# Memory between attention and mixer laid out anew, the first mixer weights split beside the last projection tiles, half of a combine moved into the attention

## The chip, the core and the metric

The kernel runs on one core of a Trainium2 chip. The metric is the device time of one execution in microseconds. Its engines are TensorE (PE in the profile; its weight loads are PEld), VectorE (DVE), ScalarE (ACT), GpSimd (POOL) and SyncE (SP, which only issues transfers here).

## What is computed

One layer of a decoder for 2048 tokens of width 1024. Four groups of heads read the same normalised input (RWKV, mLSTM, sliding-window attention and forgetting attention), one output projection follows, then a gated MLP whose gate goes through a causal convolution of width 3 ahead of the GELU. Cut to the steps after the head groups:

```python
h = concat(rwkv, mlstm, swa, fox) @ w_out          # output projection
x = x + rmsnorm(h, norm_mix_post)
u = rmsnorm(x, norm_ffn_pre)
g, up = split(u @ w_up)                            # 1024 -> 2 x 2816
f = gelu_tanh(causal_conv3(g)) * up
x = x + rmsnorm(f @ w_down, norm_ffn_post)
```

## The kernel before

Products are computed in pairs of float16 numbers (a high and a low part, three matmuls for one), so each operand is split: ACT writes the high part, DVE the rest. The scale of a split is a power of two from the largest absolute value, which is found by a maximum on DVE and an all-reduce over the partitions on POOL.

The stages that matter here are four. **Attention** (`fox`): forgetting attention, block by block; ACT's queue loads the keys into a rotating set of buffers (`ka`, `kb`). **Output projection** (`o_tiles`, from line 1475): 16 tiles of 128 tokens. A tile is 96 matmuls into `psg`, evacuated by ACT, scaled by `ot` (DVE and POOL), added to `x` on POOL (`xr`), normalised, and written into `V`, the mixer's input, by transposing transfers of SP. The scheduler lets eleven of the 16 tiles run beside the attention; five are left behind its last matmul.

**Mixer, first half** (`stage_n`): 22 steps j over slices of 128 hidden columns. `up_weights(j)` loads raw (1 MB), finds its maximum, and forms on POOL the sums `S` for a fast matrix product with seven products of half blocks; `up_split(j)` writes `Wup` (high part ACT, line 1633; low part DVE, line 1634); `ffn_up(p, j)`, for the token halves p = 0 and 1, runs 7 x 12 matmuls of 128x512 into `psa`, `psb`, `psc`, adds them up in `up` and `gb` (line 1654), applies convolution and GELU, multiplies with `up` on POOL (line 1688, F), stores F, and takes its maximum `mF` on DVE (line 1690). The split of the next weights is held back until the `up` add that `ffn_up` returns as its mark. `combine(p)` (from line 1546) prepares the block sums T of the mixer's input for half p: eight iterations of four additions on POOL, four subtractions on DVE, a cast on ACT and a subtraction on DVE.

**Mixer, second half** (`ffn_down`): 2112 matmuls with `Wd` and the stored F, scaled with the maxima `mD` of the down weights (line 1618, one load of `rd` and one reduction for each of 22 slices) and `mF`.

Each engine executes its queue in order. The order within a queue is set by a scheduler that goes by readiness; a wait for another engine holds what stands behind it on the same engine. In the kernel before, W0 and W1 are split once the pools of the output projection are closed, `raw` and `S` come from a pool of one buffer, and the 22 reductions `mD` stand in `up_weights`, with nothing that holds them back, so that DVE runs them early in the mixer.

Of the kernel before, what the change touches and what calls it, by code (L numbers as in the profile page):

```python
# [139 lines left out]
class Trunk:  # L140
# [794 lines left out]
    def stage2(self):  # L935
        with ExitStack() as ck, ExitStack() as co:
# [14 lines left out]
            with ExitStack() as cf:  # L951
                self.fox_pools(cf, 8, 4, 6, 4)
# [504 lines left out]
    def o_setup(self, ctx):  # L1457
        nc = self.nc
        self.U2 = [self.u2p.tile([P, 2, KT, C], F16, name=f"V{c}") for c in range(2)] + [None] * (NC - 2)
        self.so = self.small = self.pool(ctx, "small_o", bufs=2, side="right")  # L1460
        wp = self.pool(ctx, "wo", side="right")
        self.pso2 = self.pool(ctx, "ps_g", bufs=2, space=PSUM, side="right")
        self.row(wp, "post1")
        self.grow2 = self.gain_row(wp, 1)
# [98 lines left out]
    def stage_n(self):
# [4 lines left out]
        with ExitStack() as ctx:  # L1568
            self.small = self.sn
            self.raw = self.pool(ctx, "raw_n", bufs=1)  # L1570
            self.wp = self.pool(ctx, "w_n", bufs=2)
            self.wk = self.pool(ctx, "wk_n", bufs=2)
# [2 lines left out]
            W = {}
# [3 lines left out]
            self.Tc.append(tp.tile([P, 4, 2, 4, C], F16, name="T1"))  # L1579
# [2 lines left out]
            self.combine(1, lambda n: self.U2[1][:, n % 2, 0:4].rearrange("p k t -> p (k t)").bitcast(F32).rearrange("p (o t) -> p o t", o=4), self.Tc[1])
# [228 lines left out]
```

## Time and profile before

| | |
|---|---|
| median of 3 runs | 3085.03 us (3075.78 to 3097.76) |
| the profiled execution | 3085.7 us, of it 3083.9 us from the first to the last instruction |
| granted clock of TensorE, mean | 0.935 |
| PE busy | 2753.4 us (89%) |
| DVE, ACT, POOL busy | 1704.3, 1039.7, 844.4 us |
| longest chain by engine | PE 26%, issue 10%, DVE 5%, POOL 5%, DMA 3% |

A busy share says that an engine had work, not that it was what the others waited for. That is read from the idle time in front of an instruction and from the instruction that ended it, which the views of the trace give in brackets.

### The profile page before, as it was taken

To read this page: it belongs to the slowest core of one execution; us is meant where nothing else is said; L and a number is where in the kernel's file an instruction comes from. 1 tells how busy PE (TensorE), PEld (TensorE's weight loads), DVE (VectorE), ACT (ScalarE), POOL (GpSimd) and SP (SyncE) were. 2 spreads that over 40 slices of the span, in tenths; PEclk is the share of its full clock that TensorE was granted. 3 is DMA by queue.
4 is the path that set the end of the run, shared out by engine and by line. 5 is a ranking of instruction groups with operands and counts; after the bars stand their busy time and mean duration, and the time that the engine had idled before them with its cause. 6 is when DMAs were issued, how large, how long until landed. Compare 5 with 4: busy or idle time off the path is not lost.

```text
span 3083.9 us, 45114 instructions
## 1 busy us (share of the span) xinstructions
PE 2753.4 (89%) x17401; PEld 1657.9 (54%) x17401; DVE 1704.3 (55%) x3517; ACT 1039.7 (34%) x1844; POOL 844.4 (27%) x979
## 2 busy tenths in 40 slices
PE   5898998999888995998965578999999998999998
PEld 2455776777667873776754233444444443444443
DVE  6645664777765554567756665555555554622021
ACT  4423223445431233555643222222222222622020
POOL 2433221333233421222234322333333332010110
PEclk9998998999988996999987789999999999999999
DMA  9512333445442566575444231111111111832120
GB/s 262 118 60 83 82 102 89 103 105 137 116 131 72 130 168 173 136 143 124 106 93 116 83 121 69 55 55 55 55 55 55 55 55 52 286 117 96 48 86 21
DMA packets 341400, 313.70 MB, mean 102 GB/s; under 512 B 217600, under 2 KB 271232, under 8 KB 338368
## 3 DMA queue, kind: packets, MB, share of 16 engines
q1 hardware_dynamic: 265856, 238.42, 27.8%
q10 hardware_dynamic: 75328, 72.39, 8.1%
q8 instruction: 137, 2.24, 0.3%
q14 instruction: 79, 0.65, 0.1%
HBM read 187.86 MB, written 89.56 MB: 90 GB/s over the span
## 4 chain that ended last, share of the span: by engine, by line
PE 26%; issue 10%; DVE 5%; POOL 5%; DMA 3%; ACT 1%; ACTq 0%; POOLq 0%; SPq 0%; DVEq 0%
PE psd L1746 10%; PE psb L1651 7%; PE psc L1651 4%; PE psa L1651 4%; POOL S L1610 1%; POOL F L1688 1%; DMA rd<-in_w_dn 1%; POOL raw L1610 1%; DVE mF L1690 1%; DVE up L1654 1%; DVE mD L1618 1%; DVE gb L1654 1%; DMA wdr<-in_w_dn 0%; DVE V L1558 0%; POOL xo L1761 0%
## 5 line engine op out<-in xcount | busy, mean ns | idle before, releaser
L1651 PEld LDWEIGHTS <-Wup 128*128 128x128 f16 x3696 | 366.8, 99 | 558.4 <-issue 102.1
L1746 PE MATMUL psd<-Wd,f 128*128 128x512 f16 x2112 | 458.3, 380 | 7.2 <-ACT Wd L1731 7.2
L1651 PE MATMUL psb<-T,Wup 128*128 128x512 f16 x1584 | 383.4, 391 | 61.8 <-DVE up L1654 58.1
L1746 PEld LDWEIGHTS <-f 128*128 128x128 f16 x2112 | 207.1, 98 | 258.4 <-issue 5.8
L1651 PE MATMUL psa<-V,Wup 128*128 128x512 f16 x1056 | 249.7, 384 | 34.6 <-ACT Wup L1633 30.9
L308 PE MATMUL psg<-Wo,yt 128*128 128x256 f16 x512 | 146.9, 287 | 54.6 <-DMA yt<-hl 48.5
L1666 ACT ACTIVATE X<-psa,wm 128x512 f32<-128x512 f32 x44 | 30.2, 687 | 432.1 <-DVE p L220 254.7
L299 PE MATMUL psf<-U,hi_fm 128*128 128x256 f16 x576 | 163.6, 284 | 0.0
L298 PE MATMUL psf<-U,hi_fm 128*128 128x256 f16 x576 | 163.4, 284 | 0.0
L300 PE MATMUL psf<-U,lo_fm 128*128 128x256 f16 x576 | 163.3, 283 | 0.0
L310 PE MATMUL psg<-Wo,yt 128*128 128x256 f16 x512 | 144.6, 285 | 8.8 <-DMA yt<-hl 8.8
L1690 DVE TENSOR_REDUCE mF<-F 128x2 f32<-128x1024 f32 x44 | 53.7, 1221 | 176.2 <-POOL F L1688 176.1
L309 PE MATMUL psg<-Wo,yt 128*128 128x256 f16 x512 | 147.0, 287 | 0.0
L1754 DVE TENSOR_SCALAR od<-psd,sf 128x512 f32<-128x512 f32 x16 | 12.0, 750 | 234.0 <-PE psd L1746 229.5
L309 PE MATMUL psf<-lo_fv,U 128*128 128x256 f16 (+1 forms) x512 | 135.7, 273 | 2.7 <-DVE lo_fv L286 2.7
L308 PE MATMUL psf<-hi_fv,U 128*128 128x256 f16 (+1 forms) x512 | 135.6, 273 | 1.4 <-DVE gt L873 1.4
L1366 DVE TENSOR_REDUCE fmx<-psf 128x1 f32<-128x512 f32 (+3 forms) x160 | 96.0, 606 | 72.5 <-PE psf L1363 51.3
L310 PE MATMUL psf<-hi_fv,U 128*128 128x256 f16 (+1 forms) x512 | 135.5, 273 | 0.0
L1651 PE MATMUL psc<-T,Wup 128*128 128x512 f16 x528 | 132.4, 383 | 0.0
L1400 ACT ACTIVATE fP<-psf,ln2k 128x512 f32<-128x512 f32 (+3 forms) x160 | 98.0, 626 | 87.2 <-PE psf L1396 37.6
L1651 PE MATMUL psc<-V,Wup 128*128 128x512 f16 x528 | 122.4, 382 | 1.8 <-DVE up L1654 1.5
L1654 DVE SCALAR_TENSOR_TENSOR up<-psb,wm,X 128x512 f32<-128x512 f32 x88 | 65.8, 748 | 98.1 <-PE psb L1651 97.7
(452 smaller groups left out, 5984.6 us busy)
## 6 DMA issues: line engine op xcount, KB each, us to landing
raw<-in_w_up SPq DMA_DIRECT2D x22, 1024.0 KB
fD<-F SPq DMA_DIRECT2D x44, 512.0 KB
fr<-fD SPq DMA_DIRECT2D x88, 256.0 KB
rd<-in_w_dn SPq DMA_DIRECT2D x22, 512.0 KB
wdr<-in_w_dn ACTq DMA_DIRECT2D x22, 512.0 KB
zin<-zR SPq DMA_DIRECT2D x80, 128.0 KB
ka<-kA ACTq DMA_DIRECT2D x40, 256.0 KB
wst<-in_w_cm SPq DMA_DIRECT2D x17, 512.0 KB
```

What stands on the lines that cost most here:

```text
L298: nc.tensor.matmul(ps[:, sl], lhsT=hi[:, k, n0:n0 + nn], rhs=uh[:, k, sl], start=k == 0, stop=False)
L299: nc.tensor.matmul(ps[:, sl], lhsT=hi[:, k, n0:n0 + nn], rhs=ul[:, k, sl], start=False, stop=False)
L300: nc.tensor.matmul(ps[:, sl], lhsT=lo[:, k, n0:n0 + nn], rhs=uh[:, k, sl], start=False, stop=k == KT - 1)
L308: nc.tensor.matmul(ps, lhsT=uh[:, k, sl], rhs=hi[:, k, n0:n0 + nn], start=k == 0, stop=False)
L309: nc.tensor.matmul(ps, lhsT=uh[:, k, sl], rhs=lo[:, k, n0:n0 + nn], start=False, stop=False)
L310: nc.tensor.matmul(ps, lhsT=ul[:, k, sl], rhs=hi[:, k, n0:n0 + nn], start=False, stop=k == KT - 1)
L1366: nc.vector.tensor_reduce(out=mx[:, i, b:b + 1], in_=ps[:, :n], axis=AX.X, op=ALU.min)
L1400: nc.scalar.activation(out=e[:, o:], in_=ps[:, o:], func=AF.Exp, scale=-1.0, bias=self.ln2k)
L1651: nc.tensor.matmul(ps, lhsT=W[:, a, n, ks], rhs=rhs[u](b, k), start=first and k == 0 and i == 0, stop=k == 3 and i == 2, skip_group_check= ...
L1654: return nc.vector.scalar_tensor_tensor(out=out, in0=ps, scalar=un, in1=x, op0=ALU.mult, op1=ALU.add)
L1690: nc.vector.tensor_reduce(out=self.mF[:, 2 * p:2 * p + 2, j:j + 1], in_=F, axis=AX.X, op=ALU.max, apply_absolute_value=True)
L1746: nc.tensor.matmul(ps, lhsT=f[:, a, sl], rhs=Wd[j][:, b, ns], start=j == 0 and k == 0, stop=j == NF - 1 and k == 2)
```

## The change

It gives buffers of the mixer places of their own. `raw`, `S` and the first weight tile (`Wup0`) come from a pool that is opened before the last eight projection tiles; so the load and the split of W0 stand beside these tiles. The other buffers of `ffn_up` are fixed tiles that alternate. For the room, the attention has 7 key buffers instead of 8, the row `post2` is loaded in `ffn_down`, and one fewer of the down weights has an early place. The first half of `combine(0)` stands in the attention, its second half behind the tiles. The maximum of the down weights is a function of its own, `down_max`, which is held back to the same mark as the split.

```diff
-                self.fox_pools(cf, 8, 4, 6, 4)
+                self.fox_pools(cf, 7, 4, 6, 4)
...
+                    if c == 2:
+                        self.combine(0, lambda n: self.ow.tile([P, 4, W], F32, name="xs"), range(2))
             ck.close()
             keep = self.pool(self.ctx, "keep_n")
-            self.row(keep, "post2")
...
-            self.Tc = [u2b.tile([P, 4, 2, 4, C], F16, name="T0")]
+            self.Tc[0].append(u2b.tile([P, 4, 2, 2, C], F16, name="T0b"))
             self.tails = {}
-            for c in range(2, NC):
-                self.o_tiles(c)
-                if c == 2:
-                    self.combine(0, lambda n: self.ow.tile([P, 4, W], F32, name="xs"), self.Tc[0])
+            na = self.pool(self.cn, "n_a")
+            self.Wt = [na.tile([P, 2, 7, C], F16, name="Wup0")]
+            self.raw = na.tile([P, 4, C], F32, name="raw"), na.tile([P, 3, C], F32, name="S")
+            self.o_tiles(2)
+            self.o_tiles(3)
+            w = self.up_weights(0)
+            self.combine(0, lambda n: self.ow.tile([P, 4, W], F32, name="xs"), range(2, 4))
+            self.W = {0: self.up_split(0, w, None)}
...
+            self.Wt.append(self.pool(ctx, "n_w").tile([P, 2, 7, C], F16, name="Wup1"))
...
+            self.up, self.gb, self.F = two("up", [P, 2, C]), two("gb", [P, 2 * C + 2]), two("F", [P, 2, C])
+            self.rd = one("rd", [P, D])
...
-            for j in range(2):
-                W[j] = self.up_weights(j)
-                W[j] = self.up_split(W[j], None)
+            W[1] = self.up_split(1, self.up_weights(1), None)
...
                 mark = self.ffn_up(1, j, W[j])
-            W[2] = self.up_split(W[2], mark)
+                self.down_max(j, mark)
+            W[2] = self.up_split(2, W[2], mark)
+            self.down_max(2, mark)
             for j in range(2, NF):
                 if j + 1 < NF:
                     W[j + 1] = self.up_weights(j + 1)
                 mark = self.ffn_up(0, j, W[j])
                 if j + 1 < NF:
-                    W[j + 1] = self.up_split(W[j + 1], mark)
+                    W[j + 1] = self.up_split(j + 1, W[j + 1], mark)
+                    self.down_max(j + 1, mark)
                 mark = self.ffn_up(1, j, W[j])
...
-        d = self.wk.tile([P, D], F32, name="rd", tag="rd", bufs=1)
+        return R, S, m
+
+    def down_max(self, j, mark):
+
+        nc, d = self.nc, self.rd
         nc.sync.dma_start(out=d, in_=self.A["w_dn"][j])
-        nc.vector.tensor_reduce(out=self.mD[:, j:j + 1], in_=d, axis=AX.X, op=ALU.max, apply_absolute_value=True)
-        return R, S, m
+        with self.tc.issue_after(mark.ins):
+            nc.vector.tensor_reduce(out=self.mD[:, j:j + 1], in_=d, axis=AX.X, op=ALU.max, apply_absolute_value=True)
...
-            Wd = [None] * 3 + [wa.tile([P, 2, D], F16, name=f"Wd{j}") for j in range(3, 19)]
+            Wd = [None] * 3 + [wa.tile([P, 2, D], F16, name=f"Wd{j}") for j in range(3, 18)]
...
             fp = self.pool(ctx, "f_d")
+            self.row(fp, "post2")
```

What the queues hold at three places follows. First DVE in a late mixer step, from the mark (the `up` add) to the low part of the next weights, before:

```order
L1654 SCALAR_TENSOR_TENSOR up<-psb,wm,X 128x512
L220 TENSOR_SCALAR p_1_22960<-wm 128x1
L221 TENSOR_SCALAR p_1_22960<-p_1_22960 128x1
L222 RECIPROCAL p_1_22960<-p_1_22960 128x1
L1630 TENSOR_TENSOR wm<-p_1_22960,ug 128x1
L1654 SCALAR_TENSOR_TENSOR gb<-psb,wm,X 128x512
L1654 SCALAR_TENSOR_TENSOR gb<-psc,wm,gb 128x512
L1634 SCALAR_TENSOR_TENSOR Wup<-raw,p_1_22960,Wup 128x2048
```

and after:

```order
L1672 SCALAR_TENSOR_TENSOR up_19202<-psb,wm,X 128x512
L220 TENSOR_SCALAR p_1_22579<-wm 128x1
L1635 TENSOR_REDUCE mD<-rd 128x1
L221 TENSOR_SCALAR p_1_22579<-p_1_22579 128x1
L1672 SCALAR_TENSOR_TENSOR gb_19214<-psb,wm,X 128x512
L222 RECIPROCAL p_1_22579<-p_1_22579 128x1
L1646 TENSOR_TENSOR wm<-p_1_22579,ug 128x1
L1672 SCALAR_TENSOR_TENSOR gb_19210<-psc,wm,gb_19210 128x512
L1650 SCALAR_TENSOR_TENSOR Wup_19194<-raw,p_1_22579,Wup_19194 128x2048
```

The reduction `mD` and one `gb` add now stand ahead of the reciprocal, which ACT's split reads. The second place is DVE at the end of a step, where the three `up` adds and the maximum of F stand; one of the two kinds of step before:

```order
L1685 SCALAR_TENSOR_TENSOR F<-gb,pc,F 128x1024
L1686 SCALAR_TENSOR_TENSOR F<-gb,pc,F 128x1024
L1654 SCALAR_TENSOR_TENSOR up<-psb,wm,X 128x512
L1690 TENSOR_REDUCE mF<-F 128x2
L1654 SCALAR_TENSOR_TENSOR up<-psc,wm,up 128x512
L1654 SCALAR_TENSOR_TENSOR up<-psb,wm,X 128x512
```

and after, as in the other kind of before:

```order
L1700 SCALAR_TENSOR_TENSOR F_19222<-gb_19214,pc,F_19222 128x1024
L1701 SCALAR_TENSOR_TENSOR F_19222<-gb_19214,pc,F_19222 128x1024
L1705 TENSOR_REDUCE mF<-F_19222 128x2
L1672 SCALAR_TENSOR_TENSOR up_19202<-psb,wm,X 128x512
L1672 SCALAR_TENSOR_TENSOR up_19202<-psc,wm,up_19202 128x512
L1672 SCALAR_TENSOR_TENSOR up_19202<-psb,wm,X 128x512
```

The maximum moved ahead of the first `up` add. The third place is POOL beside the last projection tiles, after the change; `S` and `raw` are the block sums of W0 and W1, the line 1622 is the all-reduce (of W0's maximum, then of W1's), `xs` is `combine(0)`, `ot` and `xr` belong to a projection tile:

```order
L1622 ISA wm_19125<-wm_19125 128x1
L1623 ISA
L1623 TENSOR_TENSOR raw_18011<-raw_18011 128x512
L1623 TENSOR_TENSOR S_18012<-raw_18011 128x512
L1623 TENSOR_TENSOR S_18012<-raw_18011,S_18012 128x512
L1564 TENSOR_TENSOR xs_19165<-V0_14026 128x256 x2
L1564 TENSOR_TENSOR xs_19165<-V1_14027 128x256 x2
L1623 TENSOR_TENSOR S_18012<-raw_18011 128x512
L1622 ISA
L1622 ISA wm_19234<-wm_19234 128x1
L231 ISA
L231 TENSOR_TENSOR ot1_18415<-rsq_18560,mhalf_67 128x1
```

Before, one all-reduce (W0's) stood among these tiles and W1's behind them; now W1's stands there too, ahead of the scale `ot` of a tile. On PE, 36 of the matmuls of `ffn_up(0, 0)` stand between projection tiles now (17 behind the first of the last five tiles, 19 behind the second), where all of them stood behind the last tile before.

## Rows read from the trace of the kernel before

**Rows 1.** Page: busy us of an engine, share of the span, instructions.

```profile
PE 2753.4 (89%) x17401; PEld 1657.9 (54%) x17401; DVE 1704.3 (55%) x3517; ACT 1039.7 (34%) x1844; POOL 844.4 (27%) x979
```

**Rows 2.** Stretches: us, busy us by engine (PE, PEld, DVE, ACT, POOL), PEclk, DMA share, GB/s.

```profile
1200.00:1575.00 375.00, 328.99 (x2659) 251.73 (x2659) 244.32 (x478) 215.87 (x401) 95.55 (x87) 0.91 0.54 122
...
2150.00:2200.00 50.00, 50.00 (x233) 22.70 (x232) 27.85 (x31) 12.41 (x12) 15.05 (x12) 1.00 0.14 53
2200.00:2600.00 400.00, 386.20 (x1762) 173.39 (x1760) 218.26 (x237) 108.62 (x104) 130.48 (x101) 0.99 0.15 54
```

**Rows 3.** Waits of PE, 1576 to 1850: us in total, times, longest.

```profile
PE psg L308 <- DMA yt<-hl: 37.8, 3, 18.3
PE psa L1651 <- ACT Wup L1633: 30.9, 3, 16.3
```

**Rows 4.** Waits of PE, 1850 to 2610.

```profile
PE psb L1651 <- DVE up L1654: 39.5, 11, 9.9
```

**Rows 5.** Timeline of ACT: start, us, operation, [idle before, releaser]; splits of W3 to W21.

```profile
1864.59 2.00 ACT L1633 ACTIVATE Wup<-raw,p 128x2048 f16<-128x2048 f32 x1 [4.05 <-DVE wm L1630]
...
2102.68 1.99 ACT L1633 ACTIVATE Wup<-raw,p 128x2048 f16<-128x2048 f32 x1
...
2175.41 1.99 ACT L1633 ACTIVATE Wup<-raw,p 128x2048 f16<-128x2048 f32 x1
...
2256.07 1.99 ACT L1633 ACTIVATE Wup<-raw,p 128x2048 f16<-128x2048 f32 x1
...
2337.37 1.99 ACT L1633 ACTIVATE Wup<-raw,p 128x2048 f16<-128x2048 f32 x1
...
2559.96 1.99 ACT L1633 ACTIVATE Wup<-raw,p 128x2048 f16<-128x2048 f32 x1
```

**Rows 6.** Timeline of POOL in a slow mixer step.

```profile
2275.29 0.38 POOL L1608 PARTITION_ALL_REDUCE wm<-wm  x1 [6.08 <-DVE gb L1654]
2282.32 1.25 POOL L1610 TENSOR_TENSOR raw<-raw 128x512 f32<-128x512 f32 x1 [6.65 <-issue]
```

**Rows 7.** Timeline of DVE in the same step.

```profile
2255.30 0.15 DVE L220 TENSOR_SCALAR p<-wm 128x1 f32<-128x1 f32 x1
...
2288.60 1.22 DVE L1690 TENSOR_REDUCE mF<-F 128x2 f32<-128x1024 f32 x1 [10.38 <-POOL F L1688]
2289.74 0.74 DVE L1654 SCALAR_TENSOR_TENSOR up<-psb,wm,X 128x512 f32<-128x512 f32 x1
```

**Rows 8.** Timeline of PE: first mixer matmuls, a slow step, the last dozen.

```profile
1700.15 1.03 PE L1651 MATMUL psa<-V,Wup 128*128 128x512 f16 x2 [16.34 <-ACT Wup L1633]
...
1794.08 2.75 PE L1651 MATMUL psb<-T,Wup 128*128 128x512 f16 x12
...
1821.45 1.04 PE L1651 MATMUL psa<-V,Wup 128*128 128x512 f16 x2 [4.97 <-ACT Wup L1633]
...
2290.53 4.44 PE L1651 MATMUL psb<-T,Wup 128*128 128x512 f16 x12 [2.70 <-DVE up L1654]
...
2606.39 2.75 PE L1651 MATMUL psc<-V,Wup 128*128 128x512 f16 x12
```

**Rows 9.** Timeline of DVE: end of the last projection tile; last early `mD`.

```profile
1697.28 1.22 DVE L317 TENSOR_TENSOR hl<-xr,hl 128x1024 f16<-128x1024 f32 x1 [1.17 <-ACT hl L316]
...
1862.42 1.22 DVE L1618 TENSOR_REDUCE mD<-rd 128x1 f32<-128x1024 f32 x1 [2.59 <-DMA rd<-in_w_dn]
```

**Rows 10.** Combines: groups 1576 to 1800 (busy us, mean ns); ns min/median/max of one operation.

```profile
L1556 POOL TENSOR_TENSOR V<-V 128x256 f32<-128x256 f16 x32 | 24.2, 780 | 17.9 <-DVE T L1560 12.1 <-DMA V<-hl 5.8
L1558 DVE TENSOR_TENSOR V<-V 128x256 f32<-128x256 f32 x32 | 18.9, 604 | 31.2 <-POOL V L1556 31.0
L1560 DVE TENSOR_TENSOR T<-V,T 128x1024 f16<-128x1024 f32 x8 | 11.6, 1447 | 0.0
L1558 DVE TENSOR_TENSOR xs<-xs x32: 409/425/2385, 1399.8 to 1661.9; 128x256 f32<-128x256 f32 x32
```

**Rows 11.** Timeline of PE in the attention: the wait for a key block.

```profile
1213.98 0.76 PE L1362 MATMUL psf<-ka,qa 128*128 128x512 f32 x1 [8.93 <-DMA ka<-kA]
```

More of the change, by code (lines that the diff above doesn't have):

```diff
@@ L1459, in o_setup @@
         self.U2 = [self.u2p.tile([P, 2, KT, C], F16, name=f"V{c}") for c in range(2)] + [None] * (NC - 2)
+        self.Tc = [[self.u2p.tile([P, 4, 2, 2, C], F16, name="T0a")], []]
         self.so = self.small = self.pool(ctx, "small_o", bufs=2, side="right")
+        rp = self.pool(ctx, "wor", side="right")
+        self.row(rp, "post1")
+        self.grow2 = self.gain_row(rp, 1)
+        self.ow = self.pool(ctx, "ow", bufs=1, side="right")
         wp = self.pool(ctx, "wo", side="right")
         self.pso2 = self.pool(ctx, "ps_g", bufs=2, space=PSUM, side="right")
-        self.row(wp, "post1")
-        self.grow2 = self.gain_row(wp, 1)
         self.Wo = []
@@ L1544, in o_back, with combine @@
         return nxt
-    def combine(self, p, buf, T):
+    def combine(self, p, buf, ks):
         nc = self.nc
         B = [self.U2[2 * p + c][:, :, 4 * k:4 * k + 4] for c in range(2) for k in range(2)]
-        for k in range(4):
+        for k in ks:
+            T = self.Tc[p][k // 2]
             for t in range(0, C, W):
@@ L1569, in stage_n @@
             self.small = self.sn
[L1570 to L1572 removed]
+            self.Wt.append(self.pool(ctx, "n_w").tile([P, 2, 7, C], F16, name="Wup1"))
+            one = lambda n, shape: self.pool(ctx, "n_" + n).tile(shape, F32, name=n)
+            two = lambda n, shape: [one(n + str(i), shape) for i in range(2)]
+            self.X = one("X", [P, C])
+            self.up, self.gb, self.F = two("up", [P, 2, C]), two("gb", [P, 2 * C + 2]), two("F", [P, 2, C])
+            self.rd = one("rd", [P, D])
+            self.nup = 0
             self.psw = self.pool(ctx, "ps_w", bufs=2, space=PSUM)
             tp = self.pool(ctx, "t1_n", side="right")
[L1575 to L1579 removed]
+            W = self.W
+            W[1] = self.up_split(1, self.up_weights(1), None)
+            self.Tc[1] += [tp.tile([P, 4, 2, 2, C], F16, name=f"T1{i}") for i in range(2)]
             for j in range(2):
                 mark = self.ffn_up(0, j, W[j])
[L1582 removed]
+            self.combine(1, lambda n: self.U2[1][:, n % 2, 0:4].rearrange("p k t -> p (k t)").bitcast(F32).rearrange("p (o t) -> p o t", o=4), range(4))
             for j in range(2):
@@ L1603, in up_weights @@
         nc = self.nc
-        R = self.raw.tile([P, 4, C], F32, name="raw", tag="raw")
+        R, S = self.raw
         nc.sync.dma_start(out=R.rearrange("p s n -> p (s n)"), in_=self.A["w_up"][j])
@@ L1608, in up_weights @@
         nc.gpsimd.partition_all_reduce(m[:, 1:2], m[:, 0:1], P, RMAX)
-        S = self.raw.tile([P, 3, C], F32, name="S")
         gt = lambda o, x, y, op: nc.gpsimd.tensor_tensor(out=o, in0=x, in1=y, op=op)
@@ L1630, in up_split @@
             nc.vector.tensor_tensor(out=m[:, 2:3], in0=un, in1=self.ug[:, 1:2], op=ALU.mult)
-        W = self.wp.tile([P, 2, 7, C], F16, name="Wup")
+        W = self.Wt[j % 2]
         for o, x in ((slice(0, 4), R), (slice(4, 7), S)):
@@ L1681, in ffn_up @@
             nc.gpsimd.tensor_copy(out=self.tails[j], in_=gb[:, 2 * C:])
-        F = wk.tile([P, 2, C], F32, name="F")
         t = F.rearrange("p c n -> p (c n)")
@@ L1724, in ffn_down @@
             sd, sf = self.sd, self.sf
-            Wd = [wb.tile([P, 2, D], F16, name=f"Wd{j}") for j in range(3)] + Wd[3:] + [wb.tile([P, 2, D], F16, name=f"Wd{j}") for j in range(19, NF)]
+            Wd = [wb.tile([P, 2, D], F16, name=f"Wd{j}") for j in range(3)] + Wd[3:] + [wb.tile([P, 2, D], F16, name=f"Wd{j}") for j in range(18, NF)]
             def weights(j):
@@ L1785, in run @@
     def run(self):
-        self.cu, self.cr_, self.cf, self.c2, self.cb = (ExitStack() for n in range(5))
+        self.cu, self.cr_, self.cf, self.c2, self.cb, self.cn = (ExitStack() for n in range(6))
         self.setup()
```

18 lines of the change are left out of this document (9 added, 9 removed).

## The prediction

> **What bounds the kernel now.** I read the busy times first [rows 1]: PE works 89% of the span, so almost everything is decided by where PE waits. Then the table of stretches [rows 2]. It shows stages of different kinds. In the attention (1200 to 1575) PE is busy 329.0 of 375 us. In 2150 to 2200 it is busy 50.00 of 50: a mixer step at PE's own pace. Over 2200 to 2600 it is busy 386.2 of 400, so something else sets some of these steps. No edit touches the matmuls of the last product; I carry it over unchanged.
>
> Next the waits of PE. Between the end of the attention and the steady mixer the largest are two [rows 3]: 37.8 us for `yt`, the transposed input of a projection tile, and 30.9 us for the first weights (ACT Wup). In the steady mixer there is one kind, 39.5 us for `up` in 11 waits [rows 4].
>
> The order of the work says why. One mixer step (two `ffn_up`, 168 matmuls) is as long as the distance of two ACT splits of W. From the split of W3 (1864.59) to that of W21 (2559.96) there are 18 steps in 695.4 us, 38.6 each [rows 5]. They are of two kinds: 2102.68 to 2175.41 is two steps of 36.4 (PE's pace); 2256.07 to 2337.37 is two of 40.7. In the slow kind DVE's queue holds the second maximum `mF<-F` ahead of the `up` add. That maximum needs POOL's product F, and F stands in POOL's queue behind the all-reduce of the next weights: from the idle time ahead of the all-reduce to the next instruction, 6.08 + 0.38 + 6.65, POOL does nothing else for 13.1 us [rows 6], and three block sums follow ahead of F. `mF` then starts at 2288.60 after 10.38 us of an idle DVE, `up` at 2289.74 [rows 7], and PE goes on at 2290.53 after 2.70 us [rows 8]. PE pays twice: the dozen matmuls behind the stall lasts 4.44 us, an undisturbed one 2.75 (the row at 2606.39). In the fast kind `up` stands ahead of `mF`. So the slow step is a loop: mark (the `up` add) to split, to the next load of raw, to the all-reduce, to F, `mF`, `up`, mark.
>
> **The change part by part.**
>
> *1. Every step has the slow order, and a longer loop.* In the rows of the changed program all full steps on DVE have `mF` ahead of the three `up` adds (the order rows above show one); before about half had. POOL's order inside a step is the same, so F still stands behind the all-reduce. That alone puts 18 steps at 40.7 instead of 38.6: 18 x 2.1 = **+38 us**.
> To this comes the maximum of the down weights, `mD`. Before, 22 of them were run early; now one stands in each step right behind the mark, ahead of the reciprocal that ACT's split waits for, and a `gb` add moves ahead of the reciprocal too. Queued behind them: reciprocal, ACT split, DVE split, then SP's load of the next raw, the head of the loop. The price is in the trace, since one step of before has this very order: `mD` at 1862.42 to the split at 1864.59 is 2.17 us [rows 5, 9]; without it the first power instruction at 2255.30 to the split at 2256.07 is 0.77 [rows 5, 7]. That is **1.4 us** a step; its load waits are apart, because the next `rd` is loaded right behind the `mD` before it, a step ahead. Bounds: 0 (absorbed) to 2.2 (all of it). 18 x 1.4 = **+25 us**. A step is then 42.1, 18 steps are 758.
>
> *2. From the attention's end to W2.* Before, the last O matmul ended at 1700.15 - 16.34 = 1683.8, PE idled 16.34 us for W0, and the first use of W2 is at 1821.45 [rows 8]. Now W0 is split beside the last tiles: 36 of the 336 matmuls that precede W2 stand between O tiles, and the 16 us are gone. Against that, two all-reduces stand in POOL's queue there instead of one, the second ahead of the scale `ot` of a tile, with that tile's normalisation, transposes and later matmuls behind it. It can cost 0 to 13; I take 4, since PE waited for `yt` anyway in this stretch, 37.8 us [rows 3], and later tiles catch up. The mixer's remaining 300 matmuls at 50.00/233 = 0.215 us [rows 2] would end at 1683.8 + 4 + 64 = 1752 if nothing else waited. Something does: `combine(1)`, whose blocks the last 84 matmuls need. Its work in this stretch is 18.9 + 11.6 us on DVE and 24.2 on POOL [rows 10]; before it was drawn out to 1794 (the row at 1794.08 is the first matmul that needs all of it) by the all-reduces of W1 and W2 between its additions. Now both lie ahead of most of it. DVE reaches it when the last tile's row is normalised. Before, that was 15 us behind the last O matmul (`hl` at 1697.28 [rows 9]); now 4 later, behind a third all-reduce (13), and with the split of W1 between (two instructions of DVE and what they wait for, some 7): 1683.8 + 4 + 15 + 13 + 7 = 1723. An iteration is 30.5/8 = 3.8 us of DVE, with the mixer's adds between about 5.5; eight end at 1767. From its end to W2 before: 1821.45 - 1794.08 = 27.4, kept. W2 is used at 1794. Bounds: 1755 (PE's pace) and 1821 (no gain). Gain 27.
>
> *3. Attention.* One K buffer of eight is gone, so the fourth K load of the late blocks is issued only a few rows ahead of its use. Before, one load was waited for, 8.93 us [rows 11]. Bounds 0 and 9; I take 3. Half of `combine(0)` runs there: 16 POOL additions of 0.78 us and as many DVE subtractions [rows 10], beside a DVE busy 244 and a POOL busy 96 of 375 us [rows 2]. Hidden it costs nothing; were each addition to hold DVE on PE's path, 16 x 0.78 = 12.5. I take 2: nearer the lower end, since DVE has 131 us idle. Together **+5**. By the Trainium skill (SBUF — State Buffer, Who interferes with whom), a DVE instruction with two SBUF inputs and a GpSimd instruction that reads SBUF exclude each other for a whole instruction; by it the sum would take the 12.5 rather than 2, ten more. The trace agrees that some are held: the subtractions of this combine have a median of 425 ns and a longest of 2385 [rows 10].
>
> *4. W2 to W3.* Before 43.1 us (1821.45 to 1864.59), with a long wait for `up`. Now DVE's order in this one step has `mF` early, so PE is not held: 108 matmuls to the mark are 23.2 us at PE's pace, and some 2.5 to the split: 26. Gain 17.
>
> *5. End.* The last split to the last dozen: 2606.39 - 2559.96 = 46.4, kept, plus 1.4. The post2 row (512 KB) now is loaded as the last product begins: 0 to 3 us, I take 0 since its use is near the end. The Wo loads change place among SP's stores during the projections, far from their use: 0.
>
> **Sum.** W2 at 1794 + 5 = 1799; W3 at 1825; W21 at 2583; last dozen at 2631, against 2606.39: +24.6. The profiled execution took 3085.7 us (span 3083.9, 1.8 around it), the median is 3085.0: **3110 us**. About 1% (31 us) is what a measurement of this kernel can tell from no change; this lies just below.
>
> **Rivals.**
> *A, the sum* (chance 0.55), 3088 to 3132 with the bounds of 2 and 3.
> *B, mD is absorbed* (0.17). A step stays at 40.7: 25 less, 3085. For it: the split has had idle DVE around it. Against: the row of before that has this order.
> *C, the order does not bind* (0.10). If the slow steps came from something that the change removes, such as the early `rd` loads in SP's queue, all steps would run at 36.4: 18 x 5.7 = 103 less, 3007, faster. Against: the last early `mD` is at 1862.42 [rows 9], and steps are slow at 2214 to 2337 too.
> *D, the stretch between the stages gets worse* (0.18), the other side: the second all-reduce holds a tile its full 13 us, each later tile starts late, and combine(1) ends where it did. From W2 at 1815 on it decides: W2 at 1826 with the attention's 5 gives 3137, slower.
>
> **How the numbers follow.** Slower by over 1% (above 3116): 0.4 of A and nearly all of D, 0.22 + 0.17 = 0.39. Faster by over 1%: C and a little of B, 0.12. Within: 0.49. The range reaches from B with a W2 at 1780 (3066) to D (3138).
>
> **What would show it.** Step 1: the ACT splits of W in the steady mixer 42 us apart, DVE's `mF` with about 10 us idle before it in every step, PE waiting for `up` 18 times, about 5 us each with a slow dozen behind it. Step 2: no PE wait for W0, first use of W2 at 1794 to 1804. Step 3: a PE wait for K in 1300 to 1575, last attention matmul near 1580. Wrong would be: splits 36 to 37 apart (C), 40.7 (B), or W2 past 1815 (D).

## The result

The changed kernel takes 3131.18 us, the median of 4 runs (3120.62 to 3140.55), beside 3081.19 for the kernel before (4 runs): a ratio of 1.0152, 95% interval 1.0121 to 1.0182. It is slower by 1.5%. The time lies in the predicted range (3066 to 3138) and on the slower side, but 21 us above the 3110. The forecast was 25 us more than before and the measured change is 50, twice that; that it would stay within 1%, which I held likeliest, did not come.

The profiled execution of the changed kernel, the longest of its four, spans 3138.7 us against 3083.9. Cut at the points that the prediction used, the 54.8 us are:

| stretch | before | after | difference | predicted |
|---|---|---|---|---|
| start to the split of W3 | 1864.6 | 1830.1 | -34.5 | -39.6 |
| split of W3 to split of W21, 18 steps | 695.4 | 769.5 | +74.1 | +63 |
| split of W21 to the last dozen of `ffn_up` | 46.4 | 44.8 | -1.6 | +1.4 |
| last dozen to the end | 477.5 | 494.3 | +16.8 | 0 |

The first two rows are ACT's splits, which answer to [rows 5] (us from the start, duration, engine, instruction, idle time before it and what ended it):

```profile
1830.13 2.00 ACT L1649 ACTIVATE Wup<-raw,p 128x2048 f16<-128x2048 f32 x1 [1.28 <-DVE wm L1646]
...
2344.85 2.00 ACT L1649 ACTIVATE Wup<-raw,p 128x2048 f16<-128x2048 f32 x1 [1.28 <-DVE wm L1646]
...
2387.99 2.00 ACT L1649 ACTIVATE Wup<-raw,p 128x2048 f16<-128x2048 f32 x1 [1.28 <-DVE wm L1646]
...
2599.60 2.00 ACT L1649 ACTIVATE Wup<-raw,p 128x2048 f16<-128x2048 f32 x1 [1.36 <-DVE wm L1646]
```

(2599.60 - 1830.13)/18 is 42.75 us a step, the mean of 41.4 to 45.1; before it was 38.6, and 40.7 in the slow kind. The waits of PE from 1850 to the first product with `Wd` (total, times, longest) answer to [rows 4], where 11 waits made 39.5 us:

```profile
PE psb L1669 <- DVE up L1672: 76.8, 19, 6.8
```

One step on DVE answers to [rows 7]:

```profile
2377.93 1.22 DVE L1705 TENSOR_REDUCE mF<-F 128x2 f32<-128x1024 f32 x1 [10.80 <-POOL F L1703]
2379.07 0.74 DVE L1672 SCALAR_TENSOR_TENSOR up<-psb,wm,X 128x512 f32<-128x512 f32 x1
...
2385.18 0.75 DVE L1672 SCALAR_TENSOR_TENSOR up<-psb,wm,X 128x512 f32<-128x512 f32 x1 [4.58 <-PE psb L1669]
2385.85 0.14 DVE L220 TENSOR_SCALAR p<-wm 128x1 f32<-128x1 f32 x1
2385.91 1.21 DVE L1635 TENSOR_REDUCE mD<-rd 128x1 f32<-128x1024 f32 x1
```

and POOL in the same step answers to [rows 6]:

```profile
2355.43 2.36 POOL L1703 TENSOR_TENSOR F<-F,up 128x1024 f32<-128x1024 f32 x1
2364.55 0.38 POOL L1622 PARTITION_ALL_REDUCE wm<-wm  x1 [6.77 <-DVE gb L1672]
2371.66 1.25 POOL L1623 TENSOR_TENSOR raw<-raw 128x512 f32<-128x512 f32 x1 [6.73 <-issue]
2372.99 1.26 POOL L1623 TENSOR_TENSOR S<-raw 128x512 f32<-128x512 f32 x1
2374.34 1.26 POOL L1623 TENSOR_TENSOR S<-raw,S 128x512 f32<-128x512 f32 x1
2375.56 2.34 POOL L1703 TENSOR_TENSOR F<-F,up 128x1024 f32<-128x1024 f32 x1
```

The picture is the one forecast: in every step `mF` waits for F (9.7 to 13.4 us, 10.80 here), F stands on POOL behind the all-reduce and three sums, and PE pays some 4 us and then runs a slow dozen (2379.86 below, 5.07 us until the next dozen starts, where an undisturbed one takes 2.59):

```profile
2379.86 2.72 PE L1669 MATMUL psb<-T0a,Wup 128*128 128x512 f16 x6 [4.19 <-DVE up L1672]
2382.38 2.77 PE L1669 MATMUL psb<-T0b,Wup 128*128 128x512 f16 x6
2384.93 3.06 PE L1669 MATMUL psc<-V,Wup 128*128 128x512 f16 x12
```

The granted clock of TensorE says why the dozen is slow. Over these twelve matmuls, behind 4.19 us in which PE did nothing, it is 0.50, the lower of its two levels (1.2 GHz). Over the slow dozen of [rows 8], behind 2.70 us, it was 0.61. (Columns: stretch, its length, busy us and count of PE, PEld, DVE, ACT, POOL, granted clock, DMA share, GB/s.) Before:

```profile
2290.50:2294.90 4.40, 4.37 (x13) 1.69 (x13) 0.75 (x1) 0.00 (x0) 0.00 (x0) 0.61 0.04 16
```

and after:

```profile
2379.86:2384.90 5.04, 5.04 (x12) 1.78 (x12) 0.74 (x1) 0.00 (x0) 0.00 (x0) 0.50 0.03 13
```

The new loss is at the other end. After the last two dozens PE waits far longer for the first down weights than the 5.62 us before:

```profile
2644.44 2.75 PE L1669 MATMUL psc<-V,Wup 128*128 128x512 f16 x12
2663.23 8.13 PE L1762 MATMUL psd<-Wd,f 128*128 128x512 f16 x24 [16.04 <-ACT Wd L1747]
2673.59 5.34 PE L1762 MATMUL psd<-Wd,f 128*128 128x512 f16 x24 [2.23 <-ACT Wd L1747]
2681.76 58.61 PE L1762 MATMUL psd<-Wd,f 128*128 128x512 f16 x263 [2.83 <-ACT Wd L1747]
```

Of the 16.8 us, 10.4 are the longer way from the last dozen to the first product (18.79 against 8.37), 3.4 the two later waits (5.06 against 1.62), and 2.5 the slower pace of the products themselves (granted clock 0.65 over the first 24, 0.79 from 2681.7 to 2690.0; before 0.89 over the first 72).

### The profile page after: what moved, and what is told of

It reads as the page before. It is cut to its first block, busy times and chain, and to the rows that moved or that the text cites. A ratio compares the mean times of both kernels' runs of the same rounds, so it can differ in the third digit from the quotient of the medians.

```text
span 3138.7 us, 45022 instructions
## 1 busy us (share of the span) xinstructions
PE 2787.5 (89%) x17401; PEld 1668.8 (53%) x17401; DVE 1697.9 (54%) x3517; ACT 1041.4 (33%) x1844; POOL 801.5 (26%) x979
## 4 chain that ended last, share of the span: by engine, by line
PE 56%; issue 14%; DVE 11%; DMA 8%; POOL 7%; ACT 3%; SPq 1%; ACTq 0%; POOLq 0%; DVEq 0%
PE psd L1762 10%; PE psb L1669 8%; PE psc L1669 5%; PE psa L1669 4%; POOL S L1623 2%; PE psf L298 2%; PE psf L299 1%; POOL F L1703 1%; PE psf L300 1%; PE psf L308 1%; PE psf L310 1%; PE psf L309 1%; PE psb L682 1%; PE pss L1253 1%; PE pso L1415 1%
## 5 line engine op out<-in xcount | busy, mean ns | idle before, releaser
L1669 PEld LDWEIGHTS <-Wup 128*128 128x128 f16 x3696 | 373.5, 101 | 613.8 <-issue 192.0
L1669 PE MATMUL psa<-V,Wup 128*128 128x512 f16 x1056 | 251.2, 385 | 28.4 <-ACT Wup L1649 15.6
L1669 PE MATMUL psb<-T,Wup 128*128 128x512 f16 x792 | 190.1, 383 | 18.1 <-ACT T L1567 14.2
L1669 PE MATMUL psb<-T0a,Wup 128*128 128x512 f16 x396 | 120.9, 441 | 77.6 <-DVE up L1672 75.9
L308 PE MATMUL psg<-Wo,yt 128*128 128x256 f16 x512 | 144.7, 283 | 31.2 <-DMA yt<-hl 28.4
L1669 PE MATMUL psb<-T0b,Wup 128*128 128x512 f16 x396 | 116.4, 429 | 8.7 <-DVE T0b L1568 8.7
```

The lines of the kernel that those rows point to most:

```text
L308: nc.tensor.matmul(ps, lhsT=uh[:, k, sl], rhs=hi[:, k, n0:n0 + nn], start=k == 0, stop=False)
L1669: nc.tensor.matmul(ps, lhsT=W[:, a, n, ks], rhs=rhs[u](b, k), start=first and k == 0 and i == 0, stop=k == 3 and i == 2, skip_group_check= ...
```

## The experiments

All times are medians beside the kernel before on the same chip; "step" is the distance from the split of W3 to that of W21 in the profile, divided by 18.

| kernel | time us | ratio (95% interval) | step |
|---|---|---|---|
| changed kernel | 3131.2 | 1.0152 (1.0121 to 1.0182) | 42.75 |
| e1 changed, mF late | 3048.3 | 0.9872 (0.9845 to 0.9899) | 37.9 |
| e2 before, mF late | 3050.7 | 0.9884 (0.9843 to 0.9924) | 36.8 |
| e3 changed, mD not held | 3073.2 | 0.9969 (0.9949 to 0.9990) | 38.7 |
| e4 changed, loads late | 3132.9 | 1.0145 (1.0112 to 1.0177) | 42.6 |
| e5 changed, mF and mD behind the splits | 3160.9 | 1.0262 (1.0224 to 1.0301) | 44.5 |
| e6 changed, mD behind the splits | 3173.9 | 1.0287 (1.0251 to 1.0323) | 45.0 |
| e7 changed, down weights elsewhere | 3122.2 | 1.0127 (1.0098 to 1.0157) | 42.9 |
| e8 changed, line of the combine moved back | 3138.0 | 1.0180 (1.0150 to 1.0210) | 42.6 |
| e9 = e1 + mD behind the splits + e7 | 3027.1 | 0.9816 (0.9771 to 0.9860) | 36.8 |
| e10 = e1 + e7 | 3044.1 | 0.9882 (0.9844 to 0.9920) | 37.8 |
| e11 = e9 + e4 | 3022.1 | 0.9794 (0.9768 to 0.9819) | 36.9 |
| e12 changed, no all-reduce of the up weights | 2982.1 | 0.9667 (0.9636 to 0.9697) | 36.3 |

### Is it mF that holds the loop?

**e1** queues the maximum of a block's F behind the next block's marked add; **e2** is the same edit on the kernel before.

```diff
...
-        nc.vector.tensor_reduce(out=self.mF[:, 2 * p:2 * p + 2, j:j + 1], in_=F, axis=AX.X, op=ALU.max, apply_absolute_value=True)
+        late = self.late
+        self.late = lambda: nc.vector.tensor_reduce(out=self.mF[:, 2 * p:2 * p + 2, j:j + 1], in_=F, axis=AX.X, op=ALU.max, apply_absolute_value=True)
+        if late:
+            with self.tc.issue_after(mark.ins):
+                late()
```

> The changed kernel with one edit: the maximum mF of a block's F is queued on DVE behind the mark of the next block, so that in no step it stands ahead of the up adds. Loop theory (mF behind POOL's all-reduce holds up, and up holds PE): a step falls from 42.75 us to PE's pace, 36.3 (up to 38 if the split, now later behind mF and mD, is waited for), so 18 steps give back 85 to 116 us: 3015 to 3046 us. Rival (the step is set by something else, such as the load of raw or the split behind mD): steps stay at 41 to 43, 3100 to 3130 us.

> The kernel before with the same single edit (mF behind the next mark). Loop theory: its slow steps of 40.7 us fall to 36.3, the mean of 18 steps from 38.6 to 36.3, 41 us less: about 3040 us. Rival (the slow steps of before had another cause): no change, 3081 us.

Measured 3048.3, 83 us less than the changed kernel, and 3050.7. Every step of e1 is 37.8 to 38.4 us. PE's wait for `up` is all but gone from its waits after 1850 (one of 0.8 us is left); two short waits for the new weights are in its place:

```profile
PE psb L1671 <- ACT Wup L1651: 7.7, 18, 0.4
PE psa L1671 <- DVE Wup L1652: 6.9, 18, 0.4
```

So the place of `mF` on DVE is the whole wait for `up`, 4.9 of the 6.45 us by which a step of the changed kernel is longer than PE's pace of 36.3, and a loss of the kernel before as well. With `mF` late no difference between the two kernels is left: 3048.3 and 3050.7, on one chip. The times came 2 us above the expected range and some 10 us above the expected value.

### What does mD cost?

**e3** lets the scheduler place `mD` again:

```diff
-        with self.tc.issue_after(mark.ins):
-            nc.vector.tensor_reduce(out=self.mD[:, j:j + 1], in_=d, axis=AX.X, op=ALU.max, apply_absolute_value=True)
+        nc.vector.tensor_reduce(out=self.mD[:, j:j + 1], in_=d, axis=AX.X, op=ALU.max, apply_absolute_value=True)
```

> The changed kernel with one edit: the maxima mD of the down weights are not held behind the mark, so DVE runs them early as before; by DVE's order 9 of 18 steps then have up ahead of mF again. Theory (order of mF and price of mD make the loop's loss): the mean step falls from 42.75 to 38.6, 75 us less, against 10 to 15 us more where the 22 maxima crowd the start: 3066 to 3076 us. Rival (only the price of mD, 1.4 us a step, counts, the order does not): 25 us less, about 3106 us.

Measured 3073.2. With `mD` free the order of DVE is mixed again, as before: steps of 36.1 to 36.5, of 40.6 to 42.4, and a few between. The slow ones, 41.3 on the mean, are 1.5 below the 42.75: about that is what the held `mD` adds to a slow step. But holding it also did the larger thing: with it, the scheduler put `mF` first in all steps. The rest of the change, taken together, is no loss: with `mD` free the changed kernel is 0.3% faster than the kernel before (0.9949 to 0.9990).

### Is it the order on DVE, or the all-reduce behind it?

**e6** held `mD` behind the second DVE split of the next weights, **e5** besides it one `mF` of a step behind that split and the other behind the next marked add.

```diff
-            nc.vector.scalar_tensor_tensor(out=W[:, 1, o], in0=x, scalar=sc, in1=W[:, 0, o], op0=ALU.mult, op1=ALU.subtract)
+            self.split = nc.vector.scalar_tensor_tensor(out=W[:, 1, o], in0=x, scalar=sc, in1=W[:, 0, o], op0=ALU.mult, op1=ALU.subtract)
...
-                    self.down_max(j + 1, mark)
+                    self.down_max(j + 1, self.split)
+                self.flush(self.split if j + 1 < NF else mark)
```

(`flush` issues the `mF` that waits; that line is e5's alone.)

> The changed kernel with both reductions held behind the splits of the next weights on VectorE: the maximum mF of a block after the next block's marked up add, the maximum mD of the raw down weights after the two vector splits. In its order VectorE then has per step: powers, wm, gb, the two vector splits, mD, mF, and only then the wait for GpSimd. Theory A (the steps are slow because mF and mD stand ahead of the work that starts the split): the steps from the split of the weights 3 to that of the weights 21 fall from 42.75 to 36.3 us, as the quick steps of the kernel before (36.3 to 36.5); 18 x 6.45 = 116 us off 3131: 3010 to 3025. Rival B (only mF counts, the 37.8 us that its deferral alone left are set by the wait for the Wup split, not by mD): steps 37.5 to 38, 3043 to 3053, as with mF alone deferred.

> The changed kernel with one word changed: mD of the raw down weights is held behind the second vector split instead of behind the marked up add. The price of mD in its place was worked out as 1.65 us a step (slow steps 42.75 with it, 41.1 where it was not held). By that price alone the steps are 41.1 us and the time 3131 - 18 x 1.65 = 3101. But in the order the scheduler then also puts mF behind the two up adds of the next block (it still stands ahead of the marked add). Theory A (what counts is that PE's up adds do not wait behind mF): the steps come under 39 us, PE's wait for the up adds goes from 76.8 us to under 25, and the time is 3020 to 3065. Rival B (mF anywhere ahead of the mark costs the same): 41 us a step, 3095 to 3108.

Both went the wrong way, to 3160.9 and 3173.9, and neither theory had this. The order of e5 on POOL shows why, beside that of e1:

```profile
2318.82 1.27 POOL L1631 TENSOR_TENSOR S<-raw 128x512 f32<-128x512 f32 x1 [5.97 <-DMA raw<-in_w_up]
2326.06 0.38 POOL L1630 PARTITION_ALL_REDUCE wm<-wm  x1 [5.97 <-issue]
2333.51 1.25 POOL L1631 TENSOR_TENSOR raw<-raw 128x512 f32<-128x512 f32 x1 [7.08 <-issue]
...
2336.07 2.34 POOL L1711 TENSOR_TENSOR F<-F,up 128x1024 f32<-128x1024 f32 x1
```

In e1 the F of this half block stands ahead of S and of the all-reduce:

```profile
2289.96 2.35 POOL L1705 TENSOR_TENSOR F<-F,up 128x1024 f32<-128x1024 f32 x1 [2.16 <-ACT F L1704]
2295.09 1.27 POOL L1625 TENSOR_TENSOR S<-raw 128x512 f32<-128x512 f32 x1 [2.79 <-DMA raw<-in_w_up]
2302.45 0.38 POOL L1624 PARTITION_ALL_REDUCE wm<-wm  x1 [6.08 <-issue]
```

In e5 DVE does the two reductions and the maximum of the next raw ahead of the convolution's second step, so that F is ready later and the all-reduce goes first (read from the orders; no run sets it apart). Its `mF` then waits longer than in the changed kernel, ahead of two `gb` adds:

```profile
2338.44 1.22 DVE L1714 TENSOR_REDUCE mF<-F 128x2 f32<-128x1024 f32 x1 [12.13 <-POOL F L1711]
2339.58 0.74 DVE L1680 SCALAR_TENSOR_TENSOR gb<-psb,wm,X 128x512 f32<-128x512 f32 x1
```

and PE's wait after 1850 has another name and is larger than 76.8:

```profile
PE psb L1677 <- DVE gb L1680: 101.6, 18, 7.5
```

In e6 POOL's order is the same: F behind the all-reduce, `mF` waiting 11.8 to 15.2 us for it, mostly ahead of the two `gb` adds, and PE's waits are 93.5 us for `gb` and 22.1 for `up`.

Which add stands behind `mF` is not what counts; that any add does, while F is behind the all-reduce, is. **e12** takes the all-reduce itself away (each partition's own maximum stands in its place, so the result is not the layer's):

```diff
-        nc.gpsimd.partition_all_reduce(m[:, 1:2], m[:, 0:1], P, RMAX)
+        nc.gpsimd.tensor_copy(out=m[:, 1:2], in_=m[:, 0:1])
```

> The changed kernel with the maximum over the partitions left out where the up weights are scaled: GpSimd copies each partition's own maximum in place of the all-reduce (some 13 us of GpSimd a step with what stands idle around it). So part of the computation is missing. VectorE's order keeps mF directly ahead of the up adds in every half step. Theory A (an up add waits for mF, mF for GpSimd's product F, and that product stands on GpSimd behind the all-reduce and the sums of raw): with the all-reduce gone the same order has steps under 38.5 us, TensorE's wait for the up adds goes from 76.8 us to under 15, and the time is 3131 - 18 x 4.3 or more = 3054 or less. Rival B (the order on VectorE costs the time by itself, mF and mD ahead of the adds and the split, whatever GpSimd does): steps of 41 us and more, 3100 to 3131.

Measured 2982.1. DVE's order still has `mF` ahead of the `up` adds, and `mD` behind the mark, but `mF` now waits 3.56 us, and PE has a single wait for `up` after 1850, of 0.8 us:

```profile
2283.96 1.22 DVE L1705 TENSOR_REDUCE mF<-F 128x2 f32<-128x1024 f32 x1 [3.56 <-POOL F L1703]
2285.09 0.74 DVE L1672 SCALAR_TENSOR_TENSOR up<-psb,wm,X 128x512 f32<-128x512 f32 x1
...
2291.57 0.75 DVE L1672 SCALAR_TENSOR_TENSOR up<-psb,wm,X 128x512 f32<-128x512 f32 x1 [4.95 <-PE psb L1669]
...
2292.29 1.21 DVE L1635 TENSOR_REDUCE mD<-rd 128x1 f32<-128x1024 f32 x1
```

Steps of 36.3 us are 14 dozens of 2.59, PE's own pace. So neither `mF` first nor `mD` costs PE anything by itself: both cost only while the all-reduce makes the way from split to mark the longer one.

### The end: order, place or loads?

**e4** issues the row `post2` and the first `xo` loads behind the sixth split of `Wd`; **e7** gives `Wd0` a place beside the early loads and moves the others. First e7's edit:

```diff
-            Wd = [None] * 3 + [wa.tile([P, 2, D], F16, name=f"Wd{j}") for j in range(3, 18)]
+            Wd = [None] * 3 + [wa.tile([P, 2, D], F16, name=f"Wd{j}") for j in range(3, 15)]
...
+            w0 = s0.tile([P, 2, D], F16, name="Wd0")
...
```

and e4:

```diff
-            self.row(fp, "post2")
...
-                nc.scalar.activation(out=W[:, 0], in_=r, func=AF.Copy, scale=sd[:, 1:2])
+                hi = nc.scalar.activation(out=W[:, 0], in_=r, func=AF.Copy, scale=sd[:, 1:2])
+                if j == 5:
+                    with self.tc.issue_after(hi.ins):
+                        self.row(fp, "post2")
+                    self.xo_mark = hi
...
-                nc.scalar.dma_start(out=x, in_=self.x2[r])
+                with self.tc.issue_after(self.xo_mark.ins):
+                    nc.scalar.dma_start(out=x, in_=self.x2[r])
```

> The changed kernel with one edit: the load of the post2 row and the loads of xo (2 MB together) are issued behind the sixth split of the down weights instead of ahead of the first; ACT's order is otherwise the same. The last product starts 18.8 us behind the mixer's last dozen in the changed kernel, 8.4 before, and PE waits 21.1 us for Wd in all instead of 7.2. Theory A (these loads delay the all-reduce ahead of the last product and the loads of wdr): about 10 us less, 3121 us. Theory B (ACT's order, the first split behind a GELU and three f, and wdr buffers that wait for the last F): no change, 3131 us.

> The changed kernel with other places in memory for the down weights: the first (Wd0) stands beside the early loads, where raw and S end with the last split, instead of under the up weights that the last products still read; the twelve that stood lowest stay, the rest move up by three. In the order ScalarE then splits Wd0 right after the last F, ahead of f and of the GELU, and issues the next load of wdr behind the first two f; nothing else moves on any engine up to there. Theory A (the 14 us that the tail lost against the kernel before are the order on ScalarE that the new memory brought): PE's first wait for Wd falls from 16.0 us to about 10.5, the waits of TensorE for Wd together from 21.1 to under 13, and the time by 6 to 10 us to 3121 to 3125. Rival B (the wait is that for the maxima on GpSimd, whose all-reduce came 3 us later than before): the first wait stays over 14 us and the time at 3128 to 3134. The loop's steps stay at 42.7 us either way.

e4 took 3132.9, no change, though POOL stood idle 6.67 us ahead of the all-reduce of the maxima instead of 9.17: PE still waited 14.46 for `Wd`, and more behind it. ACT's queue shows what was in the way. In the kernel before, the split of `Wd0` followed the scales (which end the wait) within 0.62 us:

```profile
2612.95 0.72 ACT L1739 ACTIVATE f<-fr,sf 128x512 f16<-128x512 f32 x1 [10.10 <-DVE sf L1709]
2613.57 1.13 ACT L1731 ACTIVATE Wd<-wdr,sd 128x1024 f16<-128x1024 f32 x1
```

In the changed kernel:

```profile
2655.18 1.24 ACT L1699 ACTIVATE F<-gb,pc 128x1024 f32<-128x1024 f32 x1 [13.41 <-DVE sd L1721]
2656.32 1.32 ACT L1755 ACTIVATE f<-fr,sf 128x512 f16<-128x512 f32 x2
2660.29 1.06 ACT L1702 ACTIVATE F<-F 128x1024 f32<-128x1024 f32 x1 [2.65 <-DVE F L1701]
2661.42 0.72 ACT L1755 ACTIVATE f<-fr,sf 128x512 f16<-128x512 f32 x1
2662.05 1.13 ACT L1747 ACTIVATE Wd<-wdr,sd 128x1024 f16<-128x1024 f32 x1
```

and in e7:

```profile
2645.06 1.24 ACT L1699 ACTIVATE F<-gb,pc 128x1024 f32<-128x1024 f32 x1 [13.29 <-DVE sd L1722]
2646.21 1.14 ACT L1748 ACTIVATE Wd<-wdr,sd 128x1024 f16<-128x1024 f32 x1
```

The scales are there at 2655.2 in the changed kernel, but the split of `Wd0` stands behind a GELU and what it waits for, 6.9 us later. In the new layout `Wd0` lay where the last products still read weights, and the scheduler put its split last. With another place the first product comes 13.57 us behind the last dozen instead of 18.79, and last dozen to end is 488.2 us instead of 494.3. The time fell 9 us to 3122.2, with an interval that overlaps that of the changed kernel; the trace accounts for 6 of the 9. Of the 16.8, 10.7 stay: the all-reduce of the maxima still comes late, and a reload of `wdr` is waited for. **e10** puts e7's edit on e1:

> As the run before, without the edit to mD: mF queued behind the next marked add, and the down weights placed elsewhere. The two edits act in different places, so their gains should add: 3131 - 83 - 9 = 3039, steps of 37.8 us, TensorE's waits for Wd under 13 us in the tail. If the tail's gain hung on the slow loop (the load of wdr having more time before the last block), it is 3046 to 3050.

Measured 3044.1 against 3048.3 of e1 on another chip. Beside the kernel before on the same chip the ratios are 0.9882 and 0.9872, so no gain is shown; in the profiles the way from the last dozen to the end is 490.2 us against 493.4. The gain of e7 does not simply add.

### The start

**e8** moved the line of the first half of `combine(0)` out of the attention:

```diff
-                    if c == 2:
-                        self.combine(0, lambda n: self.ow.tile([P, 4, W], F32, name="xs"), range(2))
...
             self.o_tiles(2)
+            self.combine(0, lambda n: self.ow.tile([P, 4, W], F32, name="xs"), range(2))
             self.o_tiles(3)
```

> The changed kernel with one part undone: the first half of the block sums of the first pair of chunks is formed after the attention, where the kernel before formed all of them, instead of in it. Theory A (GpSimd and VectorE had room in the attention): the attention ends where it did (within 1 us), and GpSimd's and VectorE's sums, 5.9 us of GpSimd for each half, come back between the attention and the split of the weights 3: that split is 3 to 8 us later, 3131 + 5 = 3134 to 3139. Rival B (the first products wait for other things, the yt and Wup): no change, 3129 to 3133. Rival C (the sums cost the attention time, which I charged with 5 us): the attention ends 3 to 5 us sooner, and the time is no longer than 3131.

Measured 3138.0, its interval overlapping that of the changed kernel. But this undid nothing. The casts and subtractions of T0a, which end each block sum, stand in the attention in both programs; in the changed kernel the subtractions (count, ns, first and last start):

```profile
L1568 DVE TENSOR_TENSOR T0a<-xs,T0a x4: 1212/1218/1226, 1395.3 to 1487.2; 128x1024 f16<-128x1024 f32 x4
```

and in e8:

```profile
L1567 DVE TENSOR_TENSOR T0a<-xs,T0a x4: 1212/1224/1226, 1392.2 to 1483.9; 128x1024 f16<-128x1024 f32 x4
```

Here the scheduler took them at the same place, wherever the line stood. Nor had the kernel before all of these sums behind the attention, as the expectation says: of the 32 subtractions into `xs` 4 stood in it (from 1399.8), against 20 in the changed kernel. What the 16 more cost the attention is thus not measured by a run of its own.

### The versions that beat both kernels

**e9** is e1 with e7's places and `mD` behind the splits; **e11** adds e4.

> The changed kernel with three edits: mF of a block queued behind the marked up add of the next block (as in the run that deferred mF alone: steps of 37.8 us, 3048), mD behind the second vector split, and the down weights placed so that ScalarE splits Wd0 first (that edit alone took the tail's wait for Wd down and the time by about 9 us). Theory A (what stalls the loop is a reduction on VectorE that stands ahead of an up or gate add and waits for GpSimd's product behind the all-reduce; here mF stands behind the marked add, as in the 37.8 us run, and mD has left the way to the split): steps 36.3 to 37.0, as near to 14 dozens of 2.59 us as the kernel before's quick steps; 3048 - 18 x 1.1 - 9 = 3019; 3012 to 3030. Rival B (mD behind the split only moves its 1.2 us to the up add that stands next): steps stay 37.5 to 37.9, time 3035 to 3042. Rival C (holding mD behind the split was what made the two slow runs slow, wherever mF stands): steps of 40 us and more, over 3080.

> The fastest kernel so far (mF behind the next marked add, mD behind the second vector split, down weights placed elsewhere: 3027) with the row post2 and the three xo loads, 2 MB on ScalarE's queue, issued behind the sixth split of down weights instead of ahead of the last block's end. In that kernel TensorE still waits 9.6 us for the first f and 8.3 us once for a Wd split. Theory A (the 2 MB delay what the tail loads next, and the all-reduce of the maxima, which came 2.5 us sooner when the loads were moved alone): the two waits fall from 18.8 to 10 us or less, and the time to 3016 to 3022. Rival B (the loads hide behind other work, as when they were moved alone and the time did not change): 3024 to 3030.

Measured 3027.1 and 3022.1: 1.8% and 2.1% faster than before. With `mF` out of the way, `mD` behind the split is worth 1.0 us a step (37.8 to 36.8) and the time 17 us against e10 on the same chip; in e6 the same edit lost 43. e11's gain over e9 is inside the intervals of the two, which ran on different chips; its waits in the tail fell from 18.8 to 15.6 us only. What fell is the first wait, from 9.59 to 6.19, as the all-reduce of the maxima came sooner; in e9

```profile
2549.11 0.39 POOL L1723 PARTITION_ALL_REDUCE mm<-mm  x1 [9.55 <-issue]
```

and in e11

```profile
2536.95 0.39 POOL L1723 PARTITION_ALL_REDUCE mm<-mm  x1 [6.15 <-issue]
```

## Why the prediction was right, and where not

**1, the loop: right in mechanism, 11 us short.** All 18 steps had the slow order, DVE idled 9.7 to 13.4 us ahead of `mF`, and PE waited for `up` in each (18 waits of 3.1 to 6.8 us, 4.2 on the mean where the prediction said 5, and one of 0.8 behind them). The price of `mD` holds to a tenth: from the mark to the split it was 1.43 us before (2254.64 to 2256.07) and is 2.81 now (2385.18 to 2387.99), 1.38 more against the 1.4 taken. What was missed is the rest of the loop. The step shown (2344.85 to 2387.99, 43.1 us) is 2.8 longer than the slow step of before at 2256.07 to 2296.44: besides the 1.38 the way from the split to `up` is 0.55 longer (the all-reduce comes 0.5 later), and from `up` to the mark 0.84, since the dozen behind the stall runs slower, 5.07 us against 4.27 from its start to that of the next, at a granted clock of 0.50 against 0.61. The prediction kept the dozen of before behind a longer stall. Over all 18 stalls this dozen takes 3.9 to 5.1 us, 4.6 on the mean, and a step 42.75 and not 42.1. e1, e3 and e12 show the parts: `mF` behind the next mark removes the whole wait; `mD` unheld lowers a slow step by 1.5; without the all-reduce nothing of it is left. That `mD` is a price of every step, as the sum had it, holds only while this loop binds: in e12 it stands in the same place and costs nothing.

**2 and 4, from the attention to W3: the right follower, but 13 us short, and a date that luck helped.** W2 was first used at 1802.30 (predicted 1799), W3 split at 1830.1 (1825). But the attention ended 3.0 us earlier than before and not 5 later. Counted from its last matmuls, the split of W3 came 31.5 us sooner than before, where 44 were forecast (27 and 17): W2 gained 16.2 of the 27, W2 to W3 15.3 of the 17. So the two dates lie near because two errors had opposite signs. The 16 us for W0 did not vanish: PE waits 16.51 for `yt` first and 8.55 for W0, and later 12.8 once for X and 8.7 for T0b. The waits of PE from 1576 to 1850, to stand beside [rows 3]:

```profile
PE psg L308 <- DMA yt<-hl: 19.8, 2, 16.5
PE psa L1669 <- ACT Wup L1649: 15.6, 3, 8.5
PE psb L1669 <- ACT T L1567: 14.2, 3, 7.9
PE psa L1669 <- ACT X L1682: 12.8, 1, 12.8
PE psb L1669 <- DVE T0b L1568: 8.7, 1, 8.7
```

The waits for `yt` and for the weights were halved, and those for the block sums and X took a part of the gain. The step that dated W2 by the end of `combine(1)` named the right follower: its last subtraction starts at 1772.63 and takes 1.23 us (the forecast had the end at 1767), and W2 comes 28.4 us behind it (27.4).

**3, attention: the 5 us were not there.** Its last ten matmuls start at 1571.51 in the changed kernel and 1574.50 before (forecast: near 1580). In twelve profiles of the new layout this start lies between 1554.7 and 1574.6, in two of the old at 1574.5 and 1586.1. The waits for `ka` are 7.8 us in two times, in place of the one of 8.93 [rows 11], so no cost of the lost K buffer shows. By the Trainium skill (SBUF — State Buffer, Who interferes with whom), GpSimd's additions and DVE's subtractions exclude each other, which I had priced at up to 12.5. The traces agree that some are held: of the 32 subtractions 10 took 773 to 1196 ns, each beside an instruction of GpSimd, the others 408 to 426. But the longest was 2385 before [rows 10], and the attention did not get longer; e8 cannot set it apart.

**5, the end: the term that was mis-sized.** I carried the way from the last dozen to the end over unchanged, with a bound of 3 us for the loads, and it grew by 16.8. The diff showed the cause, one fewer early down weight and new places, and I priced only the loads. e7 shows that the place of `Wd0`, through the order on ACT, was 6 of the 16.8. The loads are not quite nothing: with them late, POOL's idle time ahead of the all-reduce of the maxima falls by 2.5 us in e4 and by 3.4 in e11 against e9, but in the changed kernel PE then waits for `Wd` all the same. The later reloads of `wdr` were read from the trace and not shown by a run.

**The rivals.** B (`mD` absorbed) fails on the 42.75; C fails too, since the order does bind; but the gain that it spoke of lies in the loop: 18 x (42.75 - 36.3) = 116 us, of which the kernel before lost 18 x 2.3 = 41. The time lies at the upper edge of A (3088 to 3132). D's time (3137) was closer than A's 3110, but not by its mechanism: the stretch between the stages got better.

## To carry to other kernels

A reduction that waits long for another engine should not stand in an in-order queue ahead of the adds that free PE's banks; hold it behind the next block's last add, and look at what the other engine has in front of its source (in e12, with a wait of 3.56 us, the same order cost nothing). A pin that is meant for one instruction can let the scheduler choose another order for its neighbours (`mD` unpinned, behind the mark, behind the split: steps of 38.7, 42.75, 45.0), so compare the queues of all engines after each pin, also far from the edit, and where memory is laid out anew, look at who inherits the places that are freed last.

## What was not expected of the hardware

The all-reduce over 128 partitions of one column shows 0.38 us of busy time but 12.8 to 15.9 us (22 of them in the changed kernel, median 13.7) in which POOL does nothing else (6.77 + 0.38 + 6.73 in the step above). Taking the 22 out was worth 149 us of 3131: 18 steps by 6.5 us in the loop, 117, and the rest ahead of W3. In the two profiles W3 was split at 1786.7 in e12 against 1830.1, 43 us sooner; 11 of these stood already at the end of the attention and may be chance.

A stall costs PE more than the wait. In the step shown it idles 4.19 us, and the dozen behind then takes 5.07 us instead of 2.59, at a granted clock of 0.50. Behind a long wait the addition is a smaller share: the 24 first products with `Wd` took 8.13 us behind a wait of 16.04, and 6.85 behind one of 6.19 in e11, while 24 of them at full pace are 5.2 (24 x 0.215). Over the 18 steps the granted clock was 0.94; in the loops of e1 and e12, where PE is not held, it is 1.00.

The time up to the end of the attention moves by up to 20 us from one profile to another of programs that are alike there (1554.7 to 1574.6), more than the 3 to 5 us that the terms for the attention were about: a difference of that size in this stretch can't be read from one pair of profiles.
